# A hybrid encoder trunk on one core: fewer small products and another order in the mixing stage, a retrieval begun beside the query projection, other pacing constants, and a last tile's output made by two engines

## The chip, the cores and the metric

The kernel runs on one core of one Trainium2 chip. The metric is the device time of one execution in microseconds. The core's engines run side by side: PE (TensorE, matrix products), DVE (VectorE), ACT (ScalarE), POOL (GpSimd), and SP, whose queue issues most of the transfers. Each takes its own instructions in order and waits on semaphores for the others.

## The reference

One layer over 512 tokens of width 1024, everything in float32:

```python
xn = rms_norm(h, norm_mix_g);  proj = xn @ w_in            # q, k, v | lru_in, lru_gate
attn = diff_attention(q, k, v, lam, positions)             # 4 heads of 2 x 64, softmax - lam * softmax
rec = rms_norm(bi_rglru(lru_in, lru_gate, ...), lru_norm_g)    # conv, gates, scan in both directions
h = h + concat(attn, rec) @ w_out
q = (rms_norm(h, norm_ffn_g) @ wq)                         # 8 heads, 2 halves of 64
v1, i1 = top_k(q1 @ keys1.T, 16);  v2, i2 = top_k(q2 @ keys2.T, 16)
sc, pos = top_k(v1 + v2 over 16 x 16, 16);  g = softmax(sc)     # 16 of 16384 experts a head
h = h + sum_k gelu(xn2 . exp_u[idx]) * g * exp_v[idx]
gate = sigmoid(rms_norm(h, norm_ple_g) @ w_gate)
out = rms_norm(h + gate * (p @ w_proj), final_norm_g)
```

## The kernel before

The 512 tokens are four tiles of 128 (`t`). PE multiplies in reduced float32; for full precision each operand is split into a high and a low part (`split`: ACT makes the high part, DVE the low one), and `mm3` makes a product of three: high by high (line 97), low by high (98), high by low (99). So every weight or row that comes from memory costs one ACT and one DVE pass before PE can use it. Nearly all the time is in these products; PE's order is that of the program, and a scheduler places the instructions of every engine.

The stages, in order of time:

- **Recurrence's projections** (0–62 us, loop over `ct`, lines 277–318): eight column tiles; `ct` 0 to 3 are then convolved and give four sigmoid gates each (`psg`, line 309). `x_norm` and the row of norms `psr` (lines 282, 287) stand in `ct` 0.
- **q, k, v blocks** (62–144, loop `blk`, lines 395–445), four weight groups `w2` each, with accumulators `pst` of all four tiles. Beside them runs `recurrence()`, a generator; in the third block (v) `rec_out()` (361–389), which splits the recurrence's output `gz` into `rec`, sums its squares over the channels with small products by a matrix of ones (`psq`, line 369, two columns wide), and loads output weights (`wo_load`).
- **Attention** (144–205): `scores` (471), `exps`, `combine`, `turn`, `values`; `normed` (536) turns norms into a row by a diagonal tile `dg` and a product with ones; then the output projection `att_out` (584).
- **Query projection** (240–305, loop `hd`, lines 864–875): per head, weights `wq_load` two ahead, products, a split into `qh`, `ql`, and two steps of the generator `tg`. Each step of `topk` is one half head: five DVE operations (`max`, `max_index`, `match_replace`, `max`, `max_index`) on 128 key scores. `tg` runs tile 3 first, then 0, 1, 2.
- **U stage** (310–890, loop `j`, lines 1012–1044): 128 loads of 128 rows of `exp_u`, each with 24 products of 384 columns (tiles 0 to 2). Generators fill DVE beside it at fixed shares: `top` (the rest of top-16), `make` (`build`: pairs of one-hot tables `o`, and products `pg` that scatter the weights into a dense array `gd`), and `side` (tile 3, whose rows are gathered one by one: `uv_items`). The shares `TOP_FIRST`, `MAKE`, `SIDE_1`, `SIDE`, `SIDE_2` stand on line 43; `SIDE_1` holds until tile 0's top-16 is done, `SIDE_2` once all tables are built.
- **V stage** (890–1430, lines 1183–1200): 128 loads of `exp_v` rows, 18 products of 512 columns each; `v_prep` (1051) multiplies gelu values by the dense weights `gc`, read back from `gd` by `weights` (988), and splits them into `ah`, `al`.
- **Finish** (1430 to the end): `finish(t)` (1138) per tile: square, norm, transposition (`turn`), split (`hl`), gate products, sigmoid, product with `pp`, square, final norm (line 1173), store. `go` (1218) orders the tiles' steps.

Of the kernel before, what the change touches and what calls it, by code (L numbers as in the profile page):

```python
# [11 lines left out]
F32 = mybir.dt.float32  # L12
# [30 lines left out]
TOP_FIRST, TOP_THEN, MAKE, SIDE_1, SIDE, BG_V, PREP, SIDE_2 = 1.9, 1.0, 0.57, 0.85, 1.2, 1.2, 60, 2.1  # L43
# [3 lines left out]
N_AT = 15, 17, 17  # L47
# [13 lines left out]
def trunk(ctx, tc, x, xT, pT, pos, w_lru, w_qkv, w_out, w_q, keys, wab, w_gate, w_proj,  # L61
# [85 lines left out]
    with ExitStack() as st:  # L147
# [129 lines left out]
        for ct in range(8):  # L277
            wh, wl = wnext
            if ct < 7:
                wnext = lru_w(ct + 1)  # L280
            if ct == 0:
                x_norm()
            ps = mm.tile([P, T], F32, tag="mm", name="ps")
            for k in range(DK):
                mm3(ps, wh[:, k, :], wl[:, k, :], xgh[:, k, :], xgl[:, k, :], k == 0, k == DK - 1)
            if ct == 0:
                psr = psb.tile([P, T], F32, tag="tr", name="psr", bufs=2)
                bcast_rows(wk, psr, [rstd[:, 0, t:t + 1] for t in range(NT)])
                nc.scalar.copy(rb, psr)
# [30 lines left out]
        late_mix = []  # L320
# [40 lines left out]
        def rec_out():  # L361
# [9 lines left out]
            nc.vector.tensor_copy(sq8[:, 0:8], psq[:, 0:8])  # L371
            rsqrt_mean(rstd[:, 1, :], sq8[:, 0:8].rearrange("p (t two) -> p t two", two=2)[:, :, 0], 512)
            nc.scalar.activation(warm, warm, AF.Exp)
            wr_ = []
            for k in range(4):
                wr_.append(wo_load(4 + k))
                yield
# [82 lines left out]
        def heads(hd):  # L460
            qkh = aw.tile([P, 2, T], R, tag="qkh", name="qkh")
            qkl = aw.tile([P, 2, T], R, tag="qkl", name="qkl")
            for s in range(2):
                pt = psb.tile([P, T], F32, tag="tr", name="pt", bufs=2)
                g = s * 4 + hd
                for t in range(NT):
                    nc.tensor.transpose(pt[:, t * P:(t + 1) * P], qk[:, t, g * P:(g + 1) * P], ident)
                split(pt, qkh[:, s, :], qkl[:, s, :])
            hq[hd] = qkh, qkl

        def scores(i):
# [9 lines left out]
            nc.vector.reduce_max(sm[:, 0:2], ps, axis=AX.X)  # L481
            nc.vector.tensor_scalar(sm[:, 2:4], sm[:, 0:2], -0.125, None, op0=ALU.mult)
            return sm, ps

        def exps(i, sm, ps):
            pe = aw.tile([P, 2, T], F32, tag="pe", name="pe", bufs=3)
            for m in range(2):
                nc.scalar.activation(pe[:, m, :], ps[:, m, :], AF.Exp, scale=0.125, bias=sm[:, 2 + m:3 + m],
# [110 lines left out]
        wq = [wq_load(hd) for hd in range(2)]  # L599
        x2h = xp.tile([P, DK, T], R, tag="xa", name="x2h")  # L600
        x2l = xp.tile([P, DK, T], R, tag="xb", name="x2l")
        for t in range(NT):
            if t == 3:
                banks.append(att_bank())
            att_out(t, banks[t], (2, 3) if t < 2 else (0, 1, 2, 3))
            for n in range(2):
# [80 lines left out]
    def topk(t, res):  # L687

        tt = slice(t * P, (t + 1) * P)
        v12 = bp.tile([P, 2, HEADS, K], F32, tag="v12", name="v12", bufs=1)  # L690
        i12 = bp.tile([P, 2, HEADS, K], U32, tag="i12", name="i12", bufs=1)
# [166 lines left out]

    def tops():
        for t in list(range(NT - 1, ND_V - 1, -1)) + list(range(ND_V)):  # L860
            yield from topk(t, res[t])

    tg = tops()
    for hd in range(HEADS):
# [9 lines left out]
        for _ in range(2 if hd else 0):  # L874
            next(tg)
    nx.close()
    bw = e0.enter_context(tc.tile_pool(name="bw", bufs=2, side="right", reuse_waits="tile"))

    pace, after = [], []
# [96 lines left out]

    JC = 8
    J0 = (P - KEEP) // JC * JC
    order = [(J0 + i) % P for i in range(P)]
    feed = [ut[j].rearrange("p k e -> p (k e)") for j in range(P)] + [v[j * P:(j + 1) * P, :] for j in order]  # L980
    ahead = []
    kept = {}

    def advance():
        while feed and len(ahead) < 3:
# [326 lines left out]
```

## Time and profile before

| | |
|---|---|
| runs, us | 1488.97, 1486.02, 1483.64 (median 1486.02) |
| profiled execution, us | 1491.43 |
| its span, us | 1489.7 |
| mean granted clock of PE | 0.993 |
| DMA | 392.64 MB, mean 264 GB/s |

Where rows below say "idle before", that engine did nothing just before the instruction; the arrow names what ended it. A duration overlaps the next one's on the same engine by some 0.08 us on DVE and 0.16 on PE, so the step from start to start is shorter than the duration shown. PE's granted clock has two levels here, 1.00 (2.4 GHz) and 0.50 (1.2 GHz); a value between is a mixture.

### The profile page before, as it was taken

To read this page: it belongs to the slowest core of one execution; us is meant where nothing else is said; L and a number is where in the kernel's file an instruction comes from. 1 tells how busy PE (TensorE), PEld (TensorE's weight loads), DVE (VectorE), ACT (ScalarE), POOL (GpSimd) and SP (SyncE) were. 2 spreads that over 40 slices of the span, in tenths; PEclk is the share of its full clock that TensorE was granted. 3 is DMA by queue.
4 is the path that set the end of the run, shared out by engine and by line. 5 is a ranking of instruction groups with operands and counts; after the bars stand their busy time and mean duration, and the time that the engine had idled before them with its cause. 6 is when DMAs were issued, how large, how long until landed. Compare 5 with 4: busy or idle time off the path is not lost.

```text
span 1489.7 us, 22160 instructions
## 1 busy us (share of the span) xinstructions
PE 1462.2 (98%) x7907; PEld 1294.2 (87%) x7907; DVE 1246.7 (84%) x2382; ACT 737.3 (49%) x1059; POOL 375.3 (25%) x320
## 2 busy tenths in 40 slices
PE   9999999999999999999999999999999999999997
PEld 7888678899999999999999997888888888888876
DVE  7686986798999998999888777888887568988896
ACT  7974654253455665556455533333333553333346
POOL 0000000002222263333433352232222004344350
PEclk9999999999999999999999999999999999999999
DMA  7134012158788899888997899899999789999962
GB/s 259 59 97 128 14 62 97 46 166 290 247 289 314 306 338 326 305 320 306 345 360 274 286 364 330 294 332 320 360 359 347 253 267 335 370 375 379 345 205 78
DMA packets 168047, 392.64 MB, mean 264 GB/s; under 512 B 15232, under 2 KB 89728, under 8 KB 164864
## 3 DMA queue, kind: packets, MB, share of 16 engines
q1 hardware_dynamic: 111760, 206.74, 41.0%
q0 software_dynamic: 38464, 140.00, 26.5%
q10 hardware_dynamic: 17712, 44.48, 7.8%
q8 instruction: 62, 1.02, 0.3%
q14 instruction: 49, 0.40, 0.1%
HBM read 344.63 MB, written 46.53 MB: 263 GB/s over the span
## 4 chain that ended last, share of the span: by engine, by line
PE 71%; DVE 14%; issue 5%; DMA 5%; ACT 4%; POOL 1%; SPq 0%; DVEq 0%; POOLq 0%; ACTq 0%
PE acc L99 11%; PE acc L98 11%; PE acc L97 11%; PE psl L97 7%; PE psl L99 7%; PE psl L98 7%; DVE rl L92 3%; PE pg L849 2%; PE ps L97 2%; PE ps L99 2%; PE ps L98 2%; DVE h L927 1%; DMA rr<-in_u_dram,qidx 1%; DMA r<-in_v_dram 1%; DVE rr L920 1%
## 5 line engine op out<-in xcount | busy, mean ns | idle before, releaser
L90 ACT ACTIVATE rh<-r 128x1024 fp32r<-128x1024 f32 x256 | 271.2, 1060 | 460.2 <-PE psl L98 190.2
L92 DVE TENSOR_TENSOR rl<-r,rh 128x1024 fp32r<-128x1024 f32 x256 | 312.4, 1221 | 104.0 <-ACT rh L90 103.3
L97 PE MATMUL psl<-x2h,rh 128*128 128x384 f32 x1024 | 346.8, 339 | 1.1 <-ACT lg L661 0.8
L99 PE MATMUL psl<-x2h,rl 128*128 128x384 f32 x1024 | 343.3, 335 | 2.6 <-DVE rl L92 2.6
L98 PE MATMUL psl<-x2l,rh 128*128 128x384 f32 x1024 | 343.0, 335 | 0.0
L97 PE MATMUL acc<-rh,ah 128*128 128x512 f32 x768 | 299.9, 391 | 2.5 <-ACT ah L90 2.5
L99 PE MATMUL acc<-rh,al 128*128 128x512 f32 x768 | 300.1, 391 | 1.2 <-DVE al L92 1.2
L98 PE MATMUL acc<-rl,ah 128*128 128x512 f32 x768 | 299.6, 390 | 0.0
L888 POOL DMA_INDIRECT rr<-in_u_dram,qidx x84 | 109.0, 1298 | 356.6 <-DVE rl L92 284.9
L99 PEld LDWEIGHTS psl<-x2h,rl 128*128 128x128 f32 x1024 | 192.4, 188 | 3.3 <-DVE rl L92 3.3
L97 PEld LDWEIGHTS psl<-x2h,rh 128*128 128x128 f32 x1024 | 192.2, 188 | 1.6 <-ACT lg L661 1.1
L98 PEld LDWEIGHTS psl<-x2l,rh 128*128 128x128 f32 x1024 | 192.6, 188 | 0.0
L888 POOL DMA_INDIRECT rr<-in_v_dram,qidxv x82 | 123.5, 1507 | 222.6 <-DVE rl L92 185.8
L97 PEld LDWEIGHTS acc<-rh,ah 128*128 128x128 f32 x768 | 144.7, 188 | 33.6 <-ACT ah L90 3.8
L99 PEld LDWEIGHTS acc<-rh,al 128*128 128x128 f32 x768 | 144.5, 188 | 32.7 <-DVE al L92 3.1
L98 PEld LDWEIGHTS acc<-rl,ah 128*128 128x128 f32 x768 | 144.6, 188 | 30.1
L920 DVE CUSTOM_DVE_ANT_0 rr<-rr,xn 128x1024 f32<-128x1024 f32 x84 | 102.0, 1217 | 8.7 <-DMA rr<-in_u_dram,qidx 8.7
L927 DVE SCALAR_TENSOR_TENSOR h<-rr,qg,h 128x1024 f32<-128x1024 f32 x82 | 104.9, 1279 | 0.1
L852 ACT COPY sg<-pg 128x512 f32<-128x512 f32 x96 | 96.0, 1109 | 6.4 <-PE pg L849 5.5
L888 POOL DMA_INDIRECT xn<-in_v_dram,qidxv x46 | 68.6, 1492 | 118.5 <-DVE rl L92 107.9
L90 ACT ACTIVATE ah<-am 128x384 fp32r<-128x384 f32 x128 | 65.6, 513 | 53.9 <-DVE am L1061 27.8
L888 POOL DMA_INDIRECT xn<-in_u_dram,qidx x44 | 62.8, 1427 | 113.0 <-DVE rl L92 82.4
(338 smaller groups left out, 2215.5 us busy)
## 6 DMA issues: line engine op xcount, KB each, us to landing
r<-in_ut_dram SPq DMA_DIRECT2D x128, 512.0 KB, 4.7
r<-in_v_dram SPq DMA_DIRECT2D x128, 512.0 KB, 6.8
gd<-sg ACTq DMA_DIRECT2D x24, 1024.0 KB, 7.8
gc<-gd SPq DMA_DIRECT2D x128, 192.0 KB, 5.0
ld<-lg ACTq DMA_DIRECT2D x98, 192.0 KB, 5.4
lg<-ld SPq DMA_DIRECT2D x98, 192.0 KB, 6.5
w<-in_w_qkv_dram SPq DMA_DIRECT2D x12, 512.0 KB, 3.6
w<-in_w_out_dram SPq DMA_DIRECT2D x8, 512.0 KB, 3.7
```

The costliest lines, as they stand in the source:

```text
L90: nc.scalar.activation(hi, src, AF.Copy, scale=1.0 if scale is None else scale)
L92: return nc.vector.tensor_sub(lo, src, hi.bitcast(F32))
L97: nc.tensor.matmul(ps, lhsT=lh, rhs=rh, start=first, stop=False)
L98: nc.tensor.matmul(ps, lhsT=lh, rhs=rl, start=False, stop=False)
L99: nc.tensor.matmul(ps, lhsT=ll, rhs=rh, start=False, stop=last)
L849: nc.tensor.matmul(pg[:, i - q, :], lhsT=o1[:, i // 2, :, i % 2], rhs=o2[part][:, i // 2, :, i % 2], start=part == 0, stop=part == 1)
L852: nc.scalar.copy(sg[:, :, s0:s0 + 4].rearrange("p j t -> p t j"), pg)
L888: g = nc.gpsimd.indirect_dma_start(out=dst, out_offset=None, in_=table, in_offset=bass.IndirectOffsetOnAxis(ap=idx, axis=0))
L920: behind(nc.vector.tensor_tensor_reduce(rr, rr, xn[:, t, :], 1.0, 0.0, ALU.mult, ALU.add, act[:, k % 16:k % 16 + 1]))
L927: behind(nc.vector.scalar_tensor_tensor(h[:, t, :], rr, qg[:, t, k:k + 1], h[:, t, :], op0=ALU.mult, op1=ALU.add))
```

## The change

- **Recurrence's projections.** `x_norm` and `psr` move from `ct` 0 to `ct` 1, and the rest of `ct` 0 runs with that of `ct` 1.
- **Row-sum of the recurrence's output.** DVE adds the four channel tiles of squares to one (1024 columns, then 512), and 4 products take the place of 16 (the profile counts two records each). They stand behind the second group of v weights.
- **Scores.** The factor -1/8 goes into the split of q (on DVE a fused operation in place of a subtraction), the maximum becomes a minimum, and 16 tiny scalings go.
- **End of the attention.** `wo_load(2)` and `(3)` stand behind `normed(2)` and `normed(3)`; the first two `wq_load`s behind the first output block; the first norms one step earlier.
- **Query projection.** Each tile has its own generator; beside the heads one half head of tile 0 runs in addition (7 in all), with two buffers for `v12` and `i12`. The code that loads U's first rows stands inside the last three heads.
- **Pacing.** `SIDE_1` 0.85 to 1.0, `SIDE_2` 2.1 to 1.6.
- **Finish.** The last tile's `h * gain` is made inside the loop for its first two column ranges; after the norm ACT scales 512 columns and DVE does two of 256.

```diff
-TOP_FIRST, TOP_THEN, MAKE, SIDE_1, SIDE, BG_V, PREP, SIDE_2 = 1.9, 1.0, 0.57, 0.85, 1.2, 1.2, 60, 2.1
+TOP_FIRST, TOP_THEN, MAKE, SIDE_1, SIDE, BG_V, PREP, SIDE_2 = 1.9, 1.0, 0.57, 1.0, 1.2, 1.2, 60, 1.6
-N_AT = 15, 17, 17
+N_AT = 14, 17, 17
...
-            if ct == 0:
+            if ct == 1:
                 x_norm()
...
+            if ct == 0:
+                first = ps
+                continue
+            if ct == 1:
+                lru_rest(0, first)
+            lru_rest(ct, ps)
...
-            psq = psb.tile([P, T], F32, tag="ro", name="psq", bufs=1)
-            for t in range(NT):
-                for ct in range(4):
-                    nc.tensor.matmul(psq[:, 2 * t:2 * t + 2], lhsT=uc[:, ct, t * P:(t + 1) * P], rhs=ones[:, 0:2],
-                                     start=ct == 0, stop=ct == 3)
...
             for k in range(4):
                 wr_.append(wo_load(4 + k))
+                if k == 0:
+                    nc.vector.tensor_add(uc[:, 0:2, :], uc[:, 0:2, :], uc[:, 2:4, :])
+                    nc.vector.tensor_add(uc[:, 0, :], uc[:, 0, :], uc[:, 1, :])
+                if k == 1:
+                    psq = psb.tile([P, T], F32, tag="ro", name="psq", bufs=1)
+                    for t in range(NT):
+                        nc.tensor.matmul(psq[:, 2 * t:2 * t + 2], lhsT=uc[:, 0, t * P:(t + 1) * P], rhs=ones[:, 0:2],
+                                         start=True, stop=True)
...
-            nc.vector.reduce_max(sm[:, 0:2], ps, axis=AX.X)
-            nc.vector.tensor_scalar(sm[:, 2:4], sm[:, 0:2], -0.125, None, op0=ALU.mult)
+            nc.vector.tensor_reduce(sm[:, 2:4], ps, axis=AX.X, op=ALU.min)
...
-        for k in (2, 3):
-            wa_.append(wo_load(k))
         normed(2)
+        wa_.append(wo_load(2))
         squares(3)
         norms(3, 4)
         normed(3)
+        wa_.append(wo_load(3))
...
         for _ in range(2 if hd else 0):
             next(tg)
+        if hd:
+            next(tks[0])
+        if hd >= HEADS - 3:
+            ahead.append(row_load(feed.pop(0)))
...
+            if nq > 2 and q < nq - 1:
+                nc.vector.tensor_mul(sg[:, ns], h[:, t, ns], gains[1][:, ns])
...
+        if nq > 2:
+            a, b, c = (slice(*x_) for x_ in cuts)
+            nc.scalar.activation(sg[:, a], sg[:, a], AF.Copy, scale=sm[:, 1:2])
+            nc.vector.scalar_tensor_tensor(sg[:, c], h[:, t, c], sm[:, 1:2], gains[1][:, c], op0=ALU.mult, op1=ALU.mult)
+            nc.vector.tensor_scalar(sg[:, b], sg[:, b], sm[:, 1:2], None, op0=ALU.mult)
```

Three places in which the order moves. **DVE at the end of the recurrence's output** (`rec`: the splits of that output; `wl2`: the low half of the second group of v weights; `wo2`: an output weight). Before:

```order
L94 SCALAR_TENSOR_TENSOR rec_1058<-ugz_93,vc_65,rec_1058 128x512
L444 TENSOR_TENSOR xn_76<-rt_1001 128x16x8
L445 TENSOR_TENSOR xn_76<-rt_1001 128x16x8
L94 SCALAR_TENSOR_TENSOR rec_1058<-ugz_93,vc_65,rec_1058 128x512 x2
L371 COPY sq8_94<-psq_1071 128x8
L92 TENSOR_TENSOR wo2_1059<-w_1093,wo2_1059 128x1024
L102 TENSOR_SCALAR rstd_75<-sq8_94 128x4
L92 TENSOR_TENSOR wl2_1100<-w2_1097,wh2_1099 128x1024
```

and now:

```order
L455 TENSOR_TENSOR xn_76<-rt_1001 128x16x8
L456 TENSOR_TENSOR xn_76<-rt_1001 128x16x8
L94 SCALAR_TENSOR_TENSOR rec_1058<-ugz_93,vc_65,rec_1058 128x512 x3
L378 TENSOR_TENSOR ugz_93<-ugz_93 128x1024
L92 TENSOR_TENSOR wl2_1080<-w2_1077,wh2_1079 128x1024
L92 TENSOR_TENSOR wo2_1059<-w_1071,wo2_1059 128x1024
L379 TENSOR_TENSOR ugz_93<-ugz_93 128x512
L92 TENSOR_TENSOR wo2_1059<-w_1107,wo2_1059 128x1024
```

The low half of the weights stood behind the copy of the row-sum and one output weight; it now stands behind three splits and the 1024-column addition. On PE the row-sum stood between the products of the first and the second group; now it stands between those of the second and the third.

**SP at the hand-over from U to V** (`gc`: the dense weights read back; `r`: a load of 128 rows). Before:

```order
L650 DMA r_9017<-in_ut_dram 128x1024
L650 DMA r_9054<-in_ut_dram 128x1024
L994 DMA gc_8986<-gd_2227 128x3x128 x6
L650 DMA r_9095<-in_ut_dram 128x1024
L994 DMA gc_8986<-gd_2227 128x3x128 x2
L650 DMA r_9132<-in_ut_dram 128x1024
L650 DMA r_9168<-in_ut_dram 128x1024
L650 DMA r_9205<-in_ut_dram 128x1024
```

and now:

```order
L662 DMA r_8966<-in_ut_dram 128x1024
L1013 DMA gc_8972<-gd_2201 128x3x128 x2
L662 DMA r_9004<-in_ut_dram 128x1024
L1013 DMA gc_8972<-gd_2201 128x3x128 x2
L662 DMA r_9040<-in_ut_dram 128x1024
L1013 DMA gc_8972<-gd_2201 128x3x128 x2
L662 DMA r_9078<-in_ut_dram 128x1024
L1013 DMA gc_8972<-gd_2201 128x3x128 x2
L662 DMA r_9115<-in_ut_dram 128x1024
L662 DMA r_9150<-in_ut_dram 128x1024
```

Six of the eight parts of the first `gc` went out in one piece; now they go two by two between four row loads.

**ACT at the last tile's square** (`x3`: its square and then its normed form; `gate`: the gate products of other tiles). Before:

```order
L1166 ACT_TABLE_LOAD
L1166 ACTIVATE sm_13930<-gate_14127 128x1
L1142 ACTIVATE x3_14075,sm_14074<-h_74 128x1024
L1161 ACT_TABLE_LOAD
L1161 ACTIVATE sg_14157<-gate_14158 128x512
L103 ACT_TABLE_LOAD
L103 ACTIVATE sm_14074<-sm_14074 128x1
L1167 ACTIVATE sg_14097,sm_13930<-h_74 128x512
L1167 ACTIVATE sg_14157,sm_14013<-h_74 128x512
```

and now:

```order
L1185 ACT_TABLE_LOAD
L1185 ACTIVATE sm_13911<-gate_14101 128x1
L1161 ACTIVATE x3_14049,sm_14048<-h_74 128x1024
L1186 ACTIVATE sg_14071,sm_13911<-h_74 128x512
L103 ACTIVATE sm_14048<-sm_14048 128x1
L1180 ACT_TABLE_LOAD
L1180 ACTIVATE sg_14131<-gate_14132 128x512
L103 ACT_TABLE_LOAD
L103 ACTIVATE sm_13911<-sm_13911 128x1
```

The sigmoid and the two table loads around it stood between the square of `h` and the root; now one square of another tile does, and the sigmoid follows the root. On PE the turn of this tile stood behind 23 of the 24 products of a gate, and now behind 8.

In the U stage, counted at the splits of row loads on DVE: ahead of the split of row 48 stood 1 accumulated side row and 12 pairs of one-hot tables, now 5 and 15. Between those of rows 118 and 130 stood 18 operations of side rows, now 15. The splits of the first three row loads stand ahead of the heads, before as now.

## Rows read from the trace of the kernel before

**Rows 1.** The page's first lines: the span, and each engine's busy time, share of the span and number of instructions.

```profile
span 1489.7 us, 22160 instructions
PE 1462.2 (98%) x7907; PEld 1294.2 (87%) x7907; DVE 1246.7 (84%) x2382; ACT 737.3 (49%) x1059; POOL 375.3 (25%) x320
```

**Rows 2.** PE's waits over the whole span: the operation that waited, who released it, then total us, times, longest us.

```profile
PE psl L99 <- DVE rl L92: 2.6, 2, 1.4
PE acc L97 <- ACT ah L90: 2.5, 3, 1.7
...
PE pb L111 <- DVE dg L110: 1.4, 2, 1.3
PE gate L97 <- DVE hl L92: 1.4, 1, 1.4
PE acc L99 <- DVE al L92: 1.2, 2, 0.6
```

**Rows 3.** The table of stretches. Columns: from:to, length, then busy us (instructions) of PE, PE's weight loads, DVE, ACT and POOL, PE's granted clock, the share of the DMA engines and GB/s.

```profile
117.40:129.00 11.60, 11.60 (x55) 10.16 (x54) 9.40 (x21) 5.17 (x6) 0.00 (x0) 0.71 0.40 137
129.00:203.00 74.00, 73.05 (x394) 53.18 (x393) 62.04 (x122) 45.97 (x102) 0.00 (x0) 1.00 0.16 52
225.00:320.00 95.00, 94.03 (x519) 84.17 (x518) 70.33 (x268) 40.40 (x63) 0.00 (x0) 1.00 0.26 88
320.00:890.00 570.00, 565.05 (x3767) 556.57 (x3766) 519.27 (x1120) 297.12 (x396) 197.12 (x128) 1.00 0.88 308
890.00:912.00 22.00, 18.71 (x72) 13.84 (x71) 14.99 (x25) 6.48 (x10) 7.38 (x7) 0.92 1.01 373
912.00:1430.00 518.00, 517.53 (x2285) 428.02 (x2284) 417.50 (x553) 201.49 (x276) 154.04 (x126) 1.00 0.94 328
```

**Rows 4.** PE in order of time at the row-sum of the recurrence's output: start, duration, line, operation.

```profile
117.42 4.72 PE L369 MATMUL psq<-ones,ugz 128*128 128x2 f32 x32
122.00 2.05 PE L97 MATMUL pst<-wh,xgh 128*128 128x512 f32 x4
```

**Rows 5.** DVE in order of time in the same place: two of the last splits of that output (`rec`), and the low half (`wl`) of the weights that PE's next products read.

```profile
119.87 1.41 DVE L94 SCALAR_TENSOR_TENSOR rec<-ugz,vc,rec 128x512 fp32r<-128x512 f32 x2
...
123.47 1.22 DVE L92 TENSOR_TENSOR wl<-w,wh 128x1024 fp32r<-128x1024 f32 x1
```

**Rows 6.** The table of stretches again (columns as in rows 3), in two places in which the granted clock is at its lower level.

```profile
119.70:126.50 6.80, 6.80 (x24) 5.83 (x24) 5.90 (x11) 2.02 (x3) 0.00 (x0) 0.50 0.25 76
908.20:911.60 3.40, 3.40 (x10) 2.65 (x9) 2.73 (x7) 1.57 (x3) 0.34 (x2) 0.50 0.98 336
```

**Rows 7.** ACT in order of time at the first gates of the recurrence: the sigmoid's table load, the load for the one-off logarithm (L244), and the load back.

```profile
33.32 1.28 ACT L312 ACT_TABLE_LOAD   x1
35.90 1.28 ACT L244 ACT_TABLE_LOAD   x1
...
37.41 1.28 ACT L312 ACT_TABLE_LOAD   x1
```

**Rows 8.** DVE's groups of instructions in 128–215: shapes and count, then busy us, mean ns of one, and idle time before them with its releaser.

```profile
L92 DVE TENSOR_TENSOR wol<-w,woh 128x1024 fp32r<-128x1024 f32 x6 | 7.3, 1224 | 5.3 <-ACT woh L90 5.3
L110 DVE TENSOR_SCALAR dg<-ident,rd 128x128 f32<-128x128 f32 x9 | 3.2, 512 | 0.6 <-PE pb L111 0.5
L482 DVE TENSOR_SCALAR sm<-sm 128x2 f32<-128x2 f32 x16 | 2.6, 161 | 0.1
```

**Rows 9.** DVE in order of time over one head of the query projection: the split of the weights, the first and the last operation of two half heads of the top-16, and the next head's split with the idle time before it.

```profile
277.36 1.23 DVE L92 TENSOR_TENSOR wl<-w,wh 128x1024 fp32r<-128x1024 f32 x1 [1.65 <-ACT wh L90]
...
279.10 0.48 DVE L700 MAX8 v<-sc 128x8 f32<-128x128 f32 x2
...
281.24 0.29 DVE L704 FIND_INDEX8 i<-v,sc 128x8 uint32<-128x128 f32 x1
...
283.18 1.23 DVE L92 TENSOR_TENSOR wl<-w,wh 128x1024 fp32r<-128x1024 f32 x1 [1.65 <-ACT wh L90]
```

**Rows 10.** SP's queue at the hand-over (start, duration of the issue, transfer), and, for the row loads in 880–910, the time from issue to landing.

```profile
893.43 2.85 SPq L650 DMA_DIRECT2D r<-in_v_dram  x1
...
DMA to landing us min/median/max: 4.7/9.8/15.6
```

**Rows 11.** DVE's groups in 320–890 (columns as in rows 8): the second operation of a pair of one-hot tables, and the accumulation of a side row.

```profile
L834 DVE TENSOR_TENSOR o<-o,sT 128x2048 f16<-128x2048 f16 x48 | 58.5, 1220 | 0.4
L927 DVE SCALAR_TENSOR_TENSOR h<-rr,qg,h 128x1024 f32<-128x1024 f32 x36 | 46.0, 1277 | 0.0
```

**Rows 12.** ACT in order of time at the last tile's square: the square, the sigmoid's table load, the root's table load.

```profile
1461.49 1.06 ACT L1142 ACTIVATE x<-h 128x1024 f32<-128x1024 f32 x1 [0.26 <-DVE h L927]
...
1462.66 1.28 ACT L1161 ACT_TABLE_LOAD   x1
...
1464.57 1.28 ACT L103 ACT_TABLE_LOAD   x1
```

**Rows 13.** PE in the same place: the turn of the last tile, and the product that then waits for its split.

```profile
1467.64 1.09 PE L1150 MATMUL turn<-ident,x 128*128 128x128 f32 x8
...
1470.38 0.50 PE L97 MATMUL gate<-wg,hl 128*128 128x512 f32 x1 [1.41 <-DVE hl L92]
```

**Rows 14.** DVE at the end: an operation on 256 columns, and the two that make the last output.

```profile
1482.31 0.43 DVE L1162 TENSOR_TENSOR sg<-sg,pp 128x256 f32<-128x256 f32 x1 [1.99 <-ACT sg L1161]
...
1485.00 1.42 DVE L1173 SCALAR_TENSOR_TENSOR sg<-h,sm,gains 128x512 f32<-128x512 f32 x2
```

More of the change, by code (lines that the diff above doesn't have):

```diff
@@ L275, in rotary, with lru_rest @@
             nc.scalar.activation(cos, ang, AF.Sin)
[L277 to L280, printed above, removed]
-            if ct == 0:
[L282 to L289, printed above, removed]
+        def lru_rest(ct, ps):
             if ct < 4:
@@ L318, in trunk @@
                     rotary()
-        late_mix = []
+        for ct in range(8):
+            wh, wl = wnext
+            if ct < 7:
+                wnext = lru_w(ct + 1)
+            if ct == 1:
+                x_norm()
+            ps = mm.tile([P, T], F32, tag="mm", name="ps")
+            for k in range(DK):
+                mm3(ps, wh[:, k, :], wl[:, k, :], xgh[:, k, :], xgl[:, k, :], k == 0, k == DK - 1)
+            if ct == 1:
+                psr = psb.tile([P, T], F32, tag="tr", name="psr", bufs=2)
+                bcast_rows(wk, psr, [rstd[:, 0, t:t + 1] for t in range(NT)])
+                nc.scalar.copy(rb, psr)
+            if ct == 0:
+                first = ps
+                continue
+            if ct == 1:
+                lru_rest(0, first)
+            lru_rest(ct, ps)
         def recurrence():
@@ L467, in heads @@
                     nc.tensor.transpose(pt[:, t * P:(t + 1) * P], qk[:, t, g * P:(g + 1) * P], ident)
-                split(pt, qkh[:, s, :], qkl[:, s, :])
+                split(pt, qkh[:, s, :], qkl[:, s, :], scale=None if s else -0.125)
             hq[hd] = qkh, qkl
@@ L605, in trunk @@
             att_out(t, banks[t], (2, 3) if t < 2 else (0, 1, 2, 3))
+            if t == 0:
+                wq = [wq_load(hd) for hd in range(2)]
             for n in range(2):
@@ L857, in trunk, with advance @@
     res = {t: [] for t in range(NT)}
+    tks = {t: topk(t, res[t]) for t in range(NT)}
     def tops():
         for t in list(range(NT - 1, ND_V - 1, -1)) + list(range(ND_V)):
-            yield from topk(t, res[t])
+            yield from tks[t]
     tg = tops()
+    pace, after = [], []
+    JC = 8
+    J0 = (P - KEEP) // JC * JC
+    order = [(J0 + i) % P for i in range(P)]
+    feed = [ut[j].rearrange("p k e -> p (k e)") for j in range(P)] + [v[j * P:(j + 1) * P, :] for j in order]
+    ahead = []
+    def advance():
+        while feed and len(ahead) < 3:
+            ahead.append(row_load(feed.pop(0)))
     for hd in range(HEADS):
@@ L875, in trunk @@
             next(tg)
+        if hd:
+            next(tks[0])
+        if hd >= HEADS - 3:
+            ahead.append(row_load(feed.pop(0)))
     nx.close()
     bw = e0.enter_context(tc.tile_pool(name="bw", bufs=2, side="right", reuse_waits="tile"))
-    pace, after = [], []
     def behind(ins):
@@ L975, in trunk @@
     top, make, side = Background(tg), Background(builds()), Background(rest())
[L977 to L981, printed above, removed]
     kept = {}
-    def advance():
-        while feed and len(ahead) < 3:
-            ahead.append(row_load(feed.pop(0)))
     def weights(c, part, vp):
```

16 lines of the change are left out of this document (8 added, 8 removed).

## The prediction

> **What bounds the kernel now.** I read the page's busy times first. PE is busy 1462.2 of 1489.7 us [rows 1], so only two things shorten the run: less PE work, or less time in which PE stands still or runs at half clock. Second come PE's waits [rows 2]; the reader is to see that they are short (none over 1.7 us) and scattered, so that no edit can find much in one place. Third is the table of stretches [rows 3], which says where time and PE's busy time part, and what else is full there. In 320–890 PE has 565.05 of 570 us, and in 912–1430 it has 517.53 of 518: there nothing is to be had but the waits. In 890–912, where the scores stage U hands over to the weighted sum V, it has 18.71 of 22 while the DMA engines are at 1.01. The views of single engines then give the prices.
>
> The profiled execution took 1491.43 us (span 1489.7), 5.4 above the median of 1486.02. The sum below is of differences read from that execution; I put it on the median. About 0.3%, 4.5 us, is what a measurement of this kernel can tell from no change.
>
> **The small products of the mixing stage.** The row-sum takes PE from 117.42 to 122.00, 4.6 us for 32 records, 0.143 each [rows 4]. The change leaves 8 records, 1.1 us, later, and gives DVE two additions, of 1024 and 512 columns. It is tempting to book 3.4 us. But the small products cover a DVE that is late: its last two splits start at 119.87 and run to 121.28, and the low half of the next weights starts at 123.47 [rows 5]. In the new order PE does four products with the high half (4 x 0.227 = 0.9, to 118.3) and then needs that low half, which stands on DVE behind three splits and the 1024-column addition. From 121.2 (the end of those splits in steps), with two operations of 1.14 us each (the step of a 1.22 us row in [rows 5]), it is there at 123.5. The gate stage gives some of it back. The one-off logarithm now stands before the first sigmoid; before, it sat between two sigmoids and cost ACT 2.8 us, from 35.90 to 38.7 [rows 7]. I take 0.8 for it at the first sigmoid, where about half of its 1.5 us of load and logarithm can fall into idle time, so that ACT's chain, which feeds the recurrence, ends 2.0 earlier: 121.5. PE's wait is then 3.2 us, and 3.2 + 1.1 replaces 4.6: **-0.3**. If the chain were held elsewhere and nothing came earlier it would be +1.7; if the recurrence is early enough for no wait, -3.5. The clock is another matter: it is at 0.50 from 119.7 to 126.5 in this place [rows 6], after a stretch of two-column products. With a wait instead of those products I leave the dip as it is; losing it would give another 2.2, half of the 4.5 us that remain at that clock after 122.0, which makes the lower bound -5.7. A second dip makes the upper bound +3.
>
> The Trainium skill ("TensorE: Matmul & The Clock Gate", Part 1, The HAM clock gate) says that an array with little to do is put to half its rate and that only activity lifts it, which speaks against trading small products for an idle array. By that rule the dip stays and the edit is worth what the sum says. The trace agrees so far, in that the 0.50 here follows two-column products and the 0.50 at 908.2 follows waits.
>
> The Trainium skill ("ScalarE: Activation LUTs", What ACT_TABLE_LOAD costs) puts a switch of function table at about 2.66 us, load and drain. The rows have 1.28 and the next instruction right behind it, and the measurement decides; by the page the one switch saved would bring ACT's chain 1.4 us earlier still, and the sum 1.4 lower.
>
> **Scores.** Sixteen tiny DVE operations (2.6 us by durations, 161 ns each) go [rows 8]; PE is busy 73.05 of 74 us there [rows 3], so at most the missing 0.95 can come back: **-0.5** (-1 to 0).
>
> **End of the attention.** Loads and splits of two output weights move behind the norm of the third head, and two weights of the query projection behind the first output block. Each split is 1.22 us on DVE and nearly the same on ACT [rows 8]. PE's two waits for the diagonal tiles are 1.4 [rows 2], and those tiles, 512 ns on average, should come sooner. But on ACT and DVE the weight splits now stand ahead of the last transposed weights, so the last value product comes up to 1.9 us later. **0** (-2 to +2.5).
>
> **Query projection.** Seven half heads of the top-16 for tile 0 are added beside the heads. On DVE a head has period 5.82 (277.36 to 283.18), with the weights' split 1.14, the query's 0.60, and two half heads of 1.18 from 279.10 to the end of the last search at 281.46, 4.1 in all, and 1.65 idle after them [rows 9]. An extra half head makes it 5.27 on average, but two heads of every pair are served together, 6.45 and 4.1. The cover is DVE's idle time, 24.7 of 95 us in 225–320 [rows 3]. PE's products are only moved. The first row splits of stage U come about two half heads late. **+0.5** (0 to +2.5).
>
> **Pacing of stage U.** With the half heads done, everything behind is earlier. Ahead of the split of row 48, DVE has four more accumulated side rows (4 x 1.20) and three more pairs of one-hot tables (6 x 1.14) than before: 11.6 us, against 8.3 taken out (7 x 1.18). The durations are 1.28 and 1.22 [rows 11]; I take the steps. PE's two waits for a row's low half (2.6 us in all, [rows 2]) fall at rows 52 and 87, and there the new order has DVE ahead by about 4 us; at rows 49 to 51 it is behind by about as much. I book the loss of some of those waits: **-1.0** (-3.5 to +4).
>
> **U to V.** The stretch 890–912 holds 72 products of 0.227, 16.3 us, and takes 22: 5.7 are lost, 3.7 of them in waits for the weighted scores' halves (2.5 + 1.2, [rows 2]), the rest at half clock in 908.2–911.6, 10 products in 3.4 us [rows 6]. Cause: transfers. Shares are 1.01 [rows 3], an issue of a row load takes 2.85 and a row lands up to 15.6 us after it [rows 10]. Now the gathered weights' loads go two by two between four row loads instead of six and two, and from row 118 to 130 there are 15 side rows, not 18. Three gathers are 3 x 0.52 MB, 4.2 us at the 373 GB/s of this stretch. **-3.5** (-5.7 to 0): with 4.2 less of transfers the waits go, and the dip behind them partly.
>
> **Tail.** PE turns the last tile after 23 of the 24 products of a gate and loses 1.4 waiting for the low half after one more [rows 13], 1.9 with the step before the turn. Now the turn stands after 8, so 16 x 0.227 = 3.6 us cover the 2.7 from turn to split. Its input must come sooner: on ACT the sigmoid with its table load and the load of the next table (1462.66 to 1465.86) stood between the square and the root [rows 12]; behind the change only the other square does. I get the turned input at 1464.6 to 1465.1, against PE at 1463.8: a wait of 0.8 to 1.3 remains, **-1.0** (-1.9 to 0). The last output took DVE 1.42 at 1485.00; now ACT scales 512 columns while DVE does two of 256 (0.43 each) [rows 14]: **-0.4**.
>
> Sum: -0.3 - 0.5 + 0 + 0.5 - 1.0 - 3.5 - 1.0 - 0.4 = **-6.2**, so 1486.0 - 6.2 = **1479.8**.
>
> **The rivals.** *The hand-over stays as it is.* For it: every queue's transfers are the same bytes, at a share of 0.94 right behind it [rows 3], so that what isn't fetched before 890 may be fetched in it. Then only 2.7 remain: 1483.3, within 0.3%. *The small products are replaced by a wait in full*, since the last splits hang on DVE and not on ACT: +1.7 and a longer dip, +1.2, in place of -0.3, 1483.0. *DVE takes over as the bound, and the run is slower.* The place is the heads to row 48. DVE is asked for 11.6 us more there, and has 7 half heads (8.3) before the rows. If none of its idle time beside the heads can be used, because PE stands in order behind the score products of tile 0 and its PSUM buffers, 8.3 go into PE's path, and the rows' lead (some 2 us at row 48) is used up by the remaining 3.3: 9.6. Such waits come in two or three pieces, and each is followed by half clock as at 908.2, 1.7 a time: twice, 13.0. That is 1479.8 + 13.0 = 1492.8, slower. It decides when a pair of heads needs more of DVE than its two periods, 11.6 us. Against it: the pair needs 10.6. *Better than booked*: no dip in the mixing stage (-2.2) and no wait there, 1475.
>
> **Chances and range.** Forecast 0.50, hand-over unchanged 0.22, wait in the mixing stage 0.08, DVE as the bound 0.09, better 0.11. Most of the forecast's own case lies below 1481.5: with the better case and a tenth of the others faster is 0.60; same 0.30; slower 0.10, which is DVE's case and a hundredth for mishaps that add up. The range 1473.5 to 1488.5 takes in the first three and nearly all of the better case, and leaves out DVE's; each end is the sum with two of its largest terms at that bound.
>
> **What would show it.** Right: in the value block, a few products into the second group of weights, a PE wait of about 3 us for their low half, with 8 small records in place of 32; no wait for the weighted scores' halves in 890–912, and PE nearer 22 busy; no wait of the gate for the split at the end; DVE fuller in 255–320 without PE waits for its halves. Wrong: DVE at its full share with PE waiting for row halves before row 50; the same 5.7 lost at the hand-over; a second stretch at 0.50 in 117–135. My forecast falls if the hand-over gives nothing.

## The result, and the profile after

The changed kernel takes 1504.99 us (median of five runs, 1502.82 to 1507.08) against 1486.02: ratio 1.0124, interval 1.0106 to 1.0141, so **1.2% slower**, some 18.4 us by the ratio. The forecast was 1479.8. The profiled execution is 1504.99, its span 1503.2.

The page's first lines, which answer to [rows 1]: PE is busy for 0.7 us less, in a span 13.5 longer.

```profile
span 1503.2 us, 22108 instructions
PE 1461.5 (97%) x7883; PEld 1293.0 (86%) x7883; DVE 1248.2 (83%) x2370; ACT 735.3 (49%) x1059; POOL 377.3 (25%) x320
```

So the loss is all waiting or half clock. PE's waits of after, as in [rows 2]: four of 3 to 7.2 us now head the list. The two waits on `ah` and `al` and the one of the gate, which the forecast shortened, are gone from its head; none of the four was in the forecast at this size.

```profile
PE psp L97 <- ACT wg L90: 7.2, 1, 7.2
PE pst L98 <- DVE wl L92: 4.9, 2, 4.7
PE psl L97 <- ACT lg L673: 4.7, 1, 4.7
PE pso L97 <- ACT wTh L90: 3.0, 1, 3.0
PE acc L97 <- ACT rh L90: 2.0, 1, 2.0
```

The table of stretches of after (columns as in [rows 3]): the hand-over is full now, while in V, where before had no loss, 8.1 and 3.5 us of PE's time are missing, and more at half clock. The first line is the value block.

```profile
119.80:123.20 3.40, 0.92 (x2) 0.83 (x3) 3.18 (x4) 1.64 (x2) 0.00 (x0) 0.50 0.52 202
...
890.00:912.00 22.00, 22.00 (x104) 18.80 (x103) 19.55 (x29) 8.98 (x14) 9.03 (x7) 1.00 1.00 363
...
1000.00:1200.00 200.00, 191.92 (x832) 157.35 (x831) 142.22 (x195) 73.91 (x104) 38.95 (x41) 0.97 0.88 306
1200.00:1430.00 230.00, 226.54 (x985) 186.39 (x984) 186.91 (x241) 87.79 (x118) 82.88 (x54) 0.99 0.95 336
```

The same stretch of V before:

```profile
1000.00:1200.00 200.00, 199.53 (x879) 164.66 (x878) 151.67 (x205) 78.51 (x109) 42.07 (x46) 1.00 0.94 325
```

**A ledger by place.** PE runs the same products in the same order but for the moved ones, so I subtract the start of a product before from the start of the same product in another execution. The table gives these offsets for after and for two experiments: e1 is the changed kernel with one constant of V changed, e2 the kernel before with that constant changed, so up to V each is a second execution of its program. The last two columns use the executions of a program that is unchanged up to that mark (before: two to five, changed: two to five): the difference of their mean offsets, changed less before, and the difference of what a stage adds, taken within each execution and then averaged. As fewer executions count further down, the last column doesn't add up exactly to the one before it. The last two rows are after alone.

| product (its start before) | after | e1 | e2 | changed less before | stage adds |
|---|---|---|---|---|---|
| end of first group, v block (117.2) | -2.0 | -1.8 | -0.3 | -1.9 | -1.9 |
| last product, v block (141.7) | 0.0 | 1.2 | -1.9 | 1.3 | +3.1 |
| last value product (208.2) | 4.0 | 4.9 | -1.9 | 5.3 | +4.0 |
| first key scores (258.6) | 0.9 | 3.3 | -4.2 | 3.8 | -1.5 |
| U, after its first row (297.1) | 2.3 | 4.7 | -4.2 | 4.6 | +1.4 |
| U, row 20 (379.6) | 7.8 | 10.7 | -4.2 | 10.3 | +5.7 |
| U, row 90 (714.2) | 4.9 | 7.9 | -1.3 | 6.2 | -4.1 |
| first V product (890.3) | 3.3 | 6.3 | -2.8 | 6.2 | -0.9 |
| V, row 6 (921.1) | -3.0 | 0.0 | -6.3 | 1.7 | -4.5 |
| V, row 58 (1133.2) | -3.0 | 0.0 | -6.3 | 1.7 | 0.0 |
| V, row 80 (1234.9) | 15.0 | 0.5 | | | +18.0 |
| last gate product (1481.6) | 13.6 | -0.9 | | | -1.3 |

Two things are to be read here. The big loss is in V, between rows 58 and 80. And a single profile is not a program: e2, with before's instructions up to V, stands 4.2 us earlier than before at 258.6 and 6.3 at 921, the stretches at half clock being shorter or absent (119.7 to 126.5 and 211.9 to 218.7 in before; 120.4 to 123.9 and none by 222 in e2). Before's profiled execution was 5.4 above its median, e2's at its median (1501.15 of 1501.24), so these places hold about what it was too long. The terms of the forecast were prices of that one execution.

**V.** The finish's weights are fetched from row 60 of V on (`PREP`): `prepare()` begins there, and its loads `w` take the four buffers `rr`, which the rows gathered for tile 3 use as well. POOL in order of time, before: the last five gathers, whose rows are still to be used, hold three buffers `xn` and two `rr`.

```profile
1123.83 1.01 POOL L888 DMA_INDIRECT xn<-in_u_dram,qidx  x1 [3.07 <-DVE rl L92]
1127.91 1.01 POOL L888 DMA_INDIRECT xn<-in_u_dram,qidx  x1 [3.07 <-DVE rl L92]
1131.99 1.01 POOL L888 DMA_INDIRECT xn<-in_u_dram,qidx  x1 [3.06 <-DVE rl L92]
1136.07 1.01 POOL L888 DMA_INDIRECT rr<-in_u_dram,qidx  x1 [3.07 <-DVE rl L92]
1140.15 1.01 POOL L888 DMA_INDIRECT rr<-in_u_dram,qidx  x1 [3.07 <-DVE rl L92]
1141.17 0.60 POOL L1112 DMA_DIRECT2D w<-in_pT_dram  x1
1141.80 0.55 POOL L1115 DMA_DIRECT2D w<-in_w_proj_dram  x1
```

And after:

```profile
1120.87 1.01 POOL L917 DMA_INDIRECT xn<-in_u_dram,qidx  x1 [3.07 <-DVE rl L92]
1124.95 1.01 POOL L917 DMA_INDIRECT xn<-in_u_dram,qidx  x1 [3.07 <-DVE rl L92]
1129.03 1.01 POOL L917 DMA_INDIRECT rr<-in_u_dram,qidx  x1 [3.07 <-DVE rl L92]
1133.11 1.01 POOL L917 DMA_INDIRECT rr<-in_u_dram,qidx  x1 [3.07 <-DVE rl L92]
1137.19 1.01 POOL L917 DMA_INDIRECT rr<-in_v_dram,qidxv  x1 [3.07 <-DVE rl L92]
1138.20 0.61 POOL L1131 DMA_DIRECT2D w<-in_pT_dram  x1
1147.67 0.55 POOL L1134 DMA_DIRECT2D w<-in_w_proj_dram  x1 [8.86 <-DVE wg L92]
```

The side rows are one ahead (the last gather is already one of `exp_v`), so the pending five are two `xn` and three `rr`: one `rr` is free instead of two. Before, two loads leave together; now each waits until the one before it has landed and been split (8.86 us). The next lines show how a late load becomes a wait of PE. ACT takes its instructions in order, and the weights' split stands ahead of V's own `ah` and `rh`; and PE's order has a product with these weights (`psp`) among V's own.

```profile
1166.76 1.06 ACT L90 ACTIVATE wg<-w 128x1024 fp32r<-128x1024 f32 x1 [7.15 <-DMA w<-in_w_proj_dram]
1167.72 0.51 ACT L90 ACTIVATE ah<-am 128x384 fp32r<-128x384 f32 x1
1168.13 1.04 ACT L90 ACTIVATE rh<-r 128x1024 fp32r<-128x1024 f32 x1
...
1239.14 1.06 ACT L90 ACTIVATE wg<-w 128x1024 fp32r<-128x1024 f32 x1 [7.00 <-DMA w<-in_w_gate_dram]
```

At the first of the two places PE stands at `psp` itself. It waits 7.21 us and then runs at half clock: 0.43 from start to start of a 512-column product, where V's products otherwise have 0.227 (199.53 us for 879 in the row of before above).

```profile
1167.87 0.80 PE L97 MATMUL psp<-wg 128*128 128x512 f32 x1 [7.21 <-ACT wg L90]
...
1169.72 0.63 PE L99 MATMUL psp<-wg,wg 128*128 128x512 f32 x1
1170.15 0.63 PE L97 MATMUL psp<-wg 128*128 128x512 f32 x1
```

The first place costs 10.8. At the second it is V's own `rh` that comes late (PE's wait of 2.0 in the list above); the waits and the half clock from 1227 to 1249 cost 7.2 more. Both together are the 18.0 of the ledger.

### The profile page after: what moved, and what is told of

Its sections match the earlier page's. It is cut to its first block, busy times and chain, and to the rows that moved or that the text cites. A ratio compares the mean times of both kernels' runs of the same rounds, so it can differ in the third digit from the quotient of the medians.

```text
span 1503.2 us, 22108 instructions
## 1 busy us (share of the span) xinstructions
PE 1461.5 (97%) x7883; PEld 1293.0 (86%) x7883; DVE 1248.2 (83%) x2370; ACT 735.3 (49%) x1059; POOL 377.3 (25%) x320
## 5 line engine op out<-in xcount | busy, mean ns | idle before, releaser
L917 POOL DMA_INDIRECT rr<-in_v_dram,qidxv x82 | 127.2, 1551 | 199.7 <-DVE rl L92 181.9
L92 DVE TENSOR_TENSOR al<-am,ah 128x384 fp32r<-128x384 f32 x128 | 70.7, 552 | 21.7 <-ACT ah L90 21.7
```

The lines of the kernel that those rows point to most:

```text
L92: return nc.vector.tensor_sub(lo, src, hi.bitcast(F32))
L917: g = nc.gpsimd.indirect_dma_start(out=dst, out_offset=None, in_=table, in_offset=bass.IndirectOffsetOnAxis(ap=idx, axis=0))
```

## The experiments

Ratios are to the kernel before, run beside the experiment on the same chip, with a median of 1484.7 to 1486.4; where experiments ran on different chips, the ratios are compared.

**e1: are the buffers the cause?** The changed kernel, preparation one row earlier.

```diff
-... BG_V, PREP, SIDE_2 = ... 1.2, 60, 1.6
+... BG_V, PREP, SIDE_2 = ... 1.2, 59, 1.6
```

> The changed kernel with one number altered: the preparation of the last stage's weights starts beside row 59 of V instead of row 60. Theory 1 (buffers): the pacing shifted the side rows by one, so that three of the five gathered rows that are pending when the preparation starts sit in the four shared row buffers, not two; one buffer is left for the twelve weight loads, they run one by one, and ACT, which splits them in order, holds the V rows behind them. That made the 18.0 us by which V fell back between 1147 and 1250 (from -3.0 to +15.0 against the kernel before). One row earlier two buffers are free again: 1504.99 - 18 = 1487, within 1484.5 to 1489.5, with no PE wait for the weights' split over 2 us. Theory 2 (transfers): the fuller pacing makes the loads of V slow as such; one row more or less changes nothing: 1503 to 1507.

1487.90 us, ratio 1.0015 (1.0002 to 1.0027): by the ratios 16.2 us come back, between the medians 17.1. POOL has the pair of loads again, and the 7.2 is gone from PE's waits:

```profile
1137.05 0.59 POOL L1131 DMA_DIRECT2D w<-in_pT_dram  x1
1137.68 0.55 POOL L1134 DMA_DIRECT2D w<-in_w_proj_dram  x1
```

**e2: the same phase in the kernel before.** Only `PREP`, 60 to 61.

> The kernel before with one number altered: the preparation starts beside row 61 of V instead of 60, so that the same five pending rows leave one shared buffer free instead of two. Theory 1 (buffers): the kernel before gets the loss of the changed one, 12 to 19 us: 1498 to 1505. Theory 2 (it is the pacing of the change): no change, 1484.5 to 1488.

1501.24 us, ratio 1.0105 (1.0087 to 1.0123), a PE wait of 6.7 for `wg`, and the serial loads:

```profile
1137.92 1.02 POOL L888 DMA_INDIRECT rr<-in_v_dram,qidxv  x1 [3.07 <-DVE rl L92]
1138.94 0.60 POOL L1112 DMA_DIRECT2D w<-in_pT_dram  x1
1148.18 0.55 POOL L1115 DMA_DIRECT2D w<-in_w_proj_dram  x1 [8.64 <-DVE wg L92]
```

With e1 this settles the main cause in both directions: none of the change's edits is needed for the loss, only the phase. In the kernels below `PREP` is set so that two buffers are free, unless the edit brings that about by itself. In the traces of all of them, as in before's and e1's, the last five gathers are three `xn` and two `rr`, the first two loads leave some 0.6 us apart, and no wait for `wg` stands among PE's; after and e2 alone have two and three, and the wait.

**e3: without the half heads** (`if hd: next(tks[0])` taken out of the changed kernel, `PREP` 60).

> The changed kernel without the seven half heads beside the query projection (they run in U as before). Its side rows come out so that two shared buffers are free when the preparation starts. Theory 1 (buffers): V's 18 us go here too; what is left tells what the half heads are worth. If they cost on balance (from the first score product to the start of V the changed kernel fell from +0.9 to +3.3): 1484 to 1486. If they pay, because without them the builds end later and the hand-over loses its 6.3 us again: 1489 to 1493. Theory 2 (transfers in V, of the pacing constants): 1500 to 1506.

1494.66 us, ratio 1.0051 (1.0037 to 1.0065): 6.8 slower than e1. Beside the heads e3 adds nothing where e1 adds 1.4, and it loses nothing by row 20 of U; it is slower later. Its profile ends 5.5 behind e1's: 1.3 of it is there at the first V product, 2.7 comes in V, where one wait (2.34 us for `rl` at 1266, with the half clock behind it) costs 4.3, and 1.5 in the tail. In e3's trace the low half stands on DVE behind an operation that waits 6.65 us for a load of the dense weights (`gc`). Why that load is late is not known, so how much of the 6.8 the half heads are worth stays open.

**e4: the old row-sum** (16 products of `ugz` by `ones`, no additions) in e1.

> The changed kernel with the preparation at row 59 and with the row-sum of the recurrence's output as before (16 small products at the old place, no additions on DVE). If the trade of small products for a wait cost the 2.0 us that PE was ahead at 115: 2 below the kernel with row 59 alone, about 1485. If, as the forecast had it, wait and products are the same: equal to that kernel within 0.7. If the saving was real: 2 to 3 above it.

1488.25 us, 1.0012 (1.0003 to 1.0021): as e1. The trade of small products for additions is neutral, within the intervals.

**e5: the old place of `wo_load(2)` and `(3)`**, ahead of `normed(2)`, in e1.

> The changed kernel with the preparation at row 59 (1487.9) and with the two output weights of the attention's end loaded ahead of the third norm, as before. Theory 1: the weights' splits stand on ACT and DVE ahead of the last transposed weights, and the wait of 3.0 us of the last value product comes from that; undone, the stretch from the first to the last value product loses the 3.3 to 3.7 us that it gained in length: 1484 to 1485.5. Theory 2: the norms' diagonal tiles are late again and take it back: 1487 to 1488.5.

1488.17 us, 1.0024 (1.0013 to 1.0035). The wait for `wTh` is 3.0 as before the edit, and ACT's order there did not move: the weights' place is not the cause.

**e9: the old scores** (factor in the exponential, maximum, 16 scalings) in e1.

```diff
-                split(pt, qkh[:, s, :], qkl[:, s, :], scale=None if s else -0.125)
+                split(pt, qkh[:, s, :], qkl[:, s, :])
...
-            nc.vector.tensor_reduce(sm[:, 2:4], ps, axis=AX.X, op=ALU.min)
+            nc.vector.reduce_max(sm[:, 0:2], ps, axis=AX.X)
+            nc.vector.tensor_scalar(sm[:, 2:4], sm[:, 0:2], -0.125, None, op0=ALU.mult)
```

> The changed kernel with the preparation at row 59 (1487.9) and with the scores as before: maximum, sixteen tiny scalings, no factor in the split of q. Undoing the order of the two output weights left the wait of the last value product at 3.0 us; in the instruction order it is the scores' edit that puts both output weights and a table load ahead of the last transposed weights on ACT. Theory 1: the wait comes from the scores' edit; without it 2.5 to 3.5 are gained, 0.5 lost to the tiny operations: 1484.5 to 1486. Theory 2: that stretch is bound by the transposed weights' own chain, and the wait stays: 1487.5 to 1489.

1485.97 us, 0.9995 (0.9981 to 1.0008), against 1.0015 for e1: by these ratios about 3 us back. ACT at the last transposed weights, in the changed kernel:

```profile
203.49 2.00 ACT L90 ACTIVATE woh<-w 128x1024 fp32r<-128x1024 f32 x2
205.51 1.28 ACT L544 ACT_TABLE_LOAD   x1
206.81 0.21 ACT L544 ACTIVATE rd<-rd 128x12 f32<-128x12 f32 x1
206.93 0.58 ACT L90 ACTIVATE wTh<-pw 128x512 fp32r<-128x512 f32 x1
```

and in e9:

```profile
203.91 1.05 ACT L90 ACTIVATE woh<-w 128x1024 fp32r<-128x1024 f32 x1
204.85 0.59 ACT L90 ACTIVATE wTh<-pw 128x512 fp32r<-128x512 f32 x1
205.46 1.28 ACT L545 ACT_TABLE_LOAD   x1
```

With the scores' edit the scheduler puts both weight splits and the root with its table ahead of the last `wTh`; PE waits 3.0 us for it in the last value products, against 0.8 in e9. An edit that takes 2.6 us off DVE made PE some 4 us later at that place, through ACT's order. Which of its three parts turned the order (factor, minimum, scalings) was not separated.

**e6, e10: the Exp of tile 0's weights in U.** ACT in the changed kernel at U's row 20, then PE:

```profile
369.70 1.28 ACT L750 ACT_TABLE_LOAD   x1 [0.39 <-issue]
377.94 0.31 ACT L750 ACTIVATE qg<-qg 128x128 f32<-128x128 f32 x1 [6.95 <-DVE qg L749]
378.15 1.04 ACT L90 ACTIVATE rh<-r 128x1024 fp32r<-128x1024 f32 x1
```

```profile
381.05 0.69 PE L97 MATMUL psl<-x2h,rh 128*128 128x384 f32 x1 [4.68 <-ACT lg L673]
```

The Exp stands at the head of ACT's queue 6.95 us before its input is there, and U's row splits and outputs stand behind it. e6 puts a pause (`yield 1.9`) ahead of it.

> The changed kernel with one pause of 1.9 (one row of U) in tile 0's top-16, ahead of the exponential of its scores; it leaves two shared buffers free at row 60. Theory 1: the exponential stands on ACT 7 us before DVE has its input, and ACT holds the next row's high half and the gelu that frees PE's accumulator: PE waits 4.7 us at 381 and runs at half clock after it. A row later the wait is short: 5 to 6 us below 1487.9, 1482 to 1483.5. Theory 2: DVE is the bound there, and PE waits for row halves instead: 1486.5 to 1489.

1488.91 us, 1.0031 (1.0017 to 1.0045). The instruction did not move and the wait stayed 4.7, so this says nothing of either theory. e10 therefore ties the Exp to the split of the next row as well.

> The changed kernel with the exponential of tile 0 bound to the row split of the next row (the pause of 1.9 alone had left ACT's order as it was); two shared buffers are free at row 60. On ACT it now stands one row's high half and one gelu later. Theory 1 (order on ACT): the wait of 4.7 us at 381 and the half clock after it go: 1482 to 1484. Theory 2 (DVE is late): PE waits for the row halves there instead, 1486.5 to 1489.

1490.38 us (1485.3 to 1500.5), 1.0033 (1.0012 to 1.0053). The Exp moved, and another instruction took its place at the head of ACT:

```profile
381.83 1.90 ACT L782 COPY sp<-d 128x2048 f16<-128x2048 f16 x1 [5.61 <-DVE d L772]
```

PE then waits 3.4 for `lg` and 2.5 for `o`. So the Exp is where the wait shows, not its cause: DVE is late at row 20, and ACT stands on whatever DVE owes it first. **e8** (row-sum and weights of before, the pause of e6, `PREP` 60) and **e11** (e9's scores with e10's edit) were to add up what was found.

> The changed kernel with the row-sum as before, the two output weights as before, and the pause ahead of the exponential; two shared buffers are free at row 60. If the three are independent: 1487.9 + 0.3 - 3.3 - 5.5 = 1479.4, 1477.5 to 1481.5, below the kernel before. If DVE is the bound in the first rows of U, or the norms take back what the weights' order gives: 1484 to 1487.

> Scores as before and the exponential one row later, in the changed kernel with two shared buffers free at row 60. If the two are independent: the sum of their gains below 1487.9, 1479 to 1482, and below the kernel before (1484.7 to 1486.3). If the rows of U are bound by DVE: 1485 to 1487.

1491.17 us, 1.0040 (1.0027 to 1.0054), and 1487.48, 1.0003 (0.9989 to 1.0017): neither is the sum of its parts.

**e7: the old late share** (`SIDE_2` 2.1, `PREP` 56) in the changed kernel.

> The changed kernel with the late share of the side rows at 2.1 as before (the early share stays at 1.0), and the preparation at row 56, which leaves two shared buffers free. The loads of the dense weights still go two by two. Theory 1 (gathers): fewer side rows ahead of the hand-over made the gain of 6.3 us between 886 and 921; with them back 4 to 6 of it is lost: 1492 to 1494. Theory 2 (spread loads): the gain comes from the two-by-two loads and stays: 1487 to 1489.

1489.67 us, 1.0025 (1.0008 to 1.0042). Against before's profile its hand-over returns 4.2 by row 6 of V instead of 6.3, and 3.1 by row 58. e2 must stand beside it: with no edit at all this stretch is 3.5 shorter there than in before's profile. The row of this stretch in e2, against 18.71 and a clock of 0.92 in [rows 3]:

```profile
890.00:912.00 22.00, 19.97 (x87) 15.94 (x86) 16.60 (x26) 7.41 (x11) 7.59 (x7) 1.00 1.03 376
```

Measured from e2, the spread loads alone give 0.7 at most, the whole change 2.8.

**e12, e13, e14: parts of the change put into the kernel before.** e12 takes `SIDE_2` 1.6 and the last output by two engines (`PREP` 63); e13 adds `SIDE_1` 1.0 (`PREP` 61); e14 is e12 with the half heads and two buffers for `v12`, `i12`, but `SIDE_1` 0.85 (`PREP` 61).

```diff
-... 0.57, 0.85, 1.2, 1.2, 60, 2.1
+... 0.57, 0.85, 1.2, 1.2, 61, 1.6
...
+    tks = {t: topk(t, res[t]) for t in range(NT)}
...
+        if hd:
+            next(tks[0])
```

> The kernel before with two parts of the change: the late share of the side rows at 1.6 and the last output made by two engines; preparation at row 63, which leaves two shared buffers free with the same pending rows. If the late share makes the gain at the hand-over: 5 to 6.5 less there and 0.5 at the end, 1479 to 1481 where the kernel before has 1486. If it takes the early share or the half heads as well: 1484 to 1486.5.

> The same with the early share at 1.0 as in the change; preparation at row 61, the same pending rows. If the early share is what costs 5 to 8 us between rows 16 and 70 of U: the hand-over's gain is spent again, 1484 to 1488. If it costs nothing: 1479 to 1481.

> The kernel before with the late share at 1.6, the last output by two engines, and the seven half heads beside the query projection, the early share at 0.85; preparation at row 61, the same pending rows. If the half heads are what makes ACT stand 7 us ahead of DVE at the exponential: 1.4 lost in the heads and 5 there, some of it won back later, 1483 to 1487. If they only move work that DVE has room for: 1478 to 1481.

e12: 1488.81 us, 1.0016 (1.0002 to 1.0029). The hand-over is full (22.00 of 22) with the late share alone, but the side rows that it puts off come up in the tail, which is 6.5 longer; the first row of its PE waits:

```profile
PE turn L1150 <- DVE x L1144: 4.0, 1, 4.0
```

e13: 1489.05 us, 1.0015 (1.0003 to 1.0027). The early share clears the tail, and costs 9.3 in U between row 20 and V (offsets -2.4 and +6.9). e14: **1483.08 us, 0.9979 (0.9967 to 0.9990)**, below both kernels, though 0.2% is less than the 0.3% that the prediction took for the limit of a measurement. The half heads cost 1.4 beside the heads and 4.7 at row 20, and 4.4 of it is back by row 90 with no larger early share; the tail is as before. The hand-over and the longest wait that is left:

```profile
890.00:912.00 22.00, 21.75 (x96) 17.64 (x95) 17.23 (x27) 8.80 (x13) 7.10 (x7) 1.00 0.98 354
```

```profile
PE psl L97 <- ACT lg L661: 3.6, 1, 3.6
```

## Why the prediction was wrong

**The step that failed** is the sentence that in 912–1430 "nothing is to be had but the waits". It was true of gains, and I let it stand for losses: the sum has no term for V. Yet the pacing edit and the half heads, both priced in the sum for other stages, together move the side rows by one, and with them the buffers that `prepare()` finds free at row 60; with the same constants and no half heads (e3) two are free there. That is +18.0 in the profile, and 16.2 of the 18.4 by the ratios of the runs (e1). None of the rivals had it. The slower one put its loss on DVE from the heads to row 48. There the changed kernel does lose, 8.4 in its profile (from 0.9 at the first key scores to 9.3 at row 48), but by row 90 4.4 of it is back, and the result doesn't come from there.

Without it the changed kernel still isn't faster (e1, +2.2 us by its ratio). The terms, in the order of the sum, each against the ledger's last column:

- **Small products**, -0.3: the first group of the v block ends 1.9 earlier and the block 1.3 later, +1.3 in all, inside the bounds. With the old row-sum (e4) the block ends no earlier, at 0.5, where the others of the changed program have 0.0 to 1.5: the trade itself is neutral, as forecast, and the +1.3 is not its price. In the working, the recurrence's end came 1.3 earlier and not 2.0: the low half that I put at 121.5 (123.5 less 2.0) was there at 122.2, and PE came for it at 117.6, not 118.3. The wait is 4.7 instead of 3.2.

DVE in order of time in that place, against [rows 5]; the weights' low half stands last:

```profile
117.87 2.08 DVE L94 SCALAR_TENSOR_TENSOR rec<-ugz,vc,rec 128x512 fp32r<-128x512 f32 x3
119.86 1.23 DVE L378 TENSOR_TENSOR ugz<-ugz 128x1024 f32<-128x1024 f32 x1
121.00 1.23 DVE L92 TENSOR_TENSOR wl<-w,wh 128x1024 fp32r<-128x1024 f32 x1
```

The clock's dip stayed, as assumed: 0.50 in the row of 119.8–123.2 above, in which PE does two products. The Trainium skill ("TensorE: Matmul & The Clock Gate", Part 1, The HAM clock gate) has it that an idle array is put to half its rate; the trace agrees.

- **Scores**, -0.5, and **end of the attention**, 0: +4.0 at the last value product, of which 1.5 comes back by the key scores, +2.5 in all. I did foresee the weight splits ahead of the last `wTh`, with 1.9 and not 3.0, but under the edit that didn't cause them, and for the scores I gave no bound on the losing side, because I counted DVE's work and not ACT's order.
- **Query projection**, +0.5: +1.4, the same in every execution with the half heads, and 0.0 in e3, which has none.
- **Pacing of U**, -1.0: +0.7, from +5.7 at row 20, -4.1 by row 90 and -0.9 by V. The waits at rows 52 and 87 are gone, as booked, and one of 1.3 for a low half stands at row 48, near the rows 49 to 51 where I had DVE behind. What the sum lacks is row 20, where tile 0's chain now ends: a wait of another kind.
- **U to V**, -3.5: -6.3 against before's profile, -4.5 against the mean, -2.8 against e2. The mechanism held and the lower share does it (e12). The price was a single execution's, and of the 3.7 of waits that I read there 3.3 lie in 890–915 (2.1 for `ah`, 1.2 for `al`).
- **Tail**, -1.0: -1.3, and the gate's wait for `hl` is gone. But it is back, at 1.2 to 1.7, in e3, e6, e8 and e10 to e14, five of which have the changed kernel's tail line for line: the gain hangs on more than that edit, probably on the side rows that are pending.
- **Last output**, -0.4: -0.1. From the reciprocal's start to the end of the span it is 4.79 us, before 4.86. ACT and DVE are done together 0.95 behind that start, where DVE alone took 1.61. But the output leaves in two stores, and before, the first left while DVE made the second half: the first now leaves no sooner (0.95 against 0.97), the second 0.3 sooner. The two stores before, then now:

```profile
1485.78 1.03 SPq L1174 DMA_DIRECT2D out_dram<-sg  x2
```

```profile
1499.39 0.81 SPq L1202 DMA_DIRECT2D out_dram<-sg  x2
```

One sum of the prediction does not come out: with its two largest terms, the small products and the hand-over, at their lower bounds the range would begin at 1472.2 and not at 1473.5. Nothing hangs on it.

Shown by experiments: the phase of the buffers (e1, e2), the scores' edit as a whole (e9), the late share (e12), the half heads as what brings the loss at row 20 (4.7 in e14, 0.0 in e3), and that the Exp is not the cause of its wait (e10). Argued from rows alone: that it is DVE's lateness by which the half heads do this, and ACT's order as the way from a late load to V's own products. Open: the late load in V of e3, and why the same program's dips fall differently from run to run, which moves a mark by up to 6.3 us. Not tried: a fifth buffer for the finish's weights, and on their own the smaller moves (`x_norm`, the first norms, `wq_load`, U's first row loads).

## What to carry to other kernels

When a pacing constant is changed, follow the paced work to its last use of every shared pool, and count the free buffers at the moment a second user comes: here one row more or less decided between 0 and 15 to 18 us, in either kernel. In an engine that works in order, look for the instruction at its head whose input comes from elsewhere (a load, a slower engine); what it holds up is the price, and an edit that only takes work off one engine may reorder another. Price no term from one execution that is well above its median: the excess is in some place, and a term may be buying it back.

## What the runs showed of the hardware

In the changed kernel each of PE's four longest waits (3.0, 4.7, 4.7 and 7.2 us) was followed by a stretch at half clock. From the end of the wait 3.1 to 6.1 us were left of that stretch, which costs 1.6 to 3.1 us more; behind the 7.21 at 1168 a product of 512 columns took 0.43 from start to start. A load of a table of ACT's functions took 1.28 us and the next instruction began right behind it (205.51, then 206.81), as before. And loads of 0.26 and 0.52 MB on POOL's queue, one at a time beside V's rows, took 5.8 to 9.5 us from one issue to the next, the landing and the split of the one before included (1138.20 to 1147.67 the longest, 1154.23 to 1159.99 the shortest of the first four). With one free buffer they could not keep up here.
